# Weight sums formed by accumulating transfers instead of VectorE, in a two-layer streaming trunk

## The chip, the cores and the metric

The kernel runs on one core of one Trainium2 chip. A time is in device microseconds (us) for one execution of the whole program; of several runs the median is given. TensorE is called PE, its weight loads PEld, VectorE DVE, ScalarE ACT, GpSimd POOL; SP is the sequencer that issues nearly all DMA transfers here.

## The reference

One sequence of 512 rows of width 2048 goes through two layers in float32. The first is an mLSTM mixer (8 heads), the second a chunked band attention (16 heads) that reads one shared K and V. Nearly all the work is matrix products of 512 rows with weights that are read once:

```
proj = h @ w_in                        # layer 1: 2048 x 20496
qk = silu(causal_conv(proj[..., :A_V0], conv_w, conv_b))
ht = mlstm_chunkwise(q, k, v, li, lf)
y = sigmoid(o) * rmsnorm(ht) * silu(z);   x = x + gate * rmsnorm(y @ w_out)
kv = hkv @ kv_w                        # 2048 x 4096, shared
qz = h @ w_in                          # layer 2: 2048 x 4096
o = chunk_band_attention(q, k, v, rel_table)
x = x + gate * rmsnorm((o * silu(z)) @ w_out)
```

## The kernel before, in words

Each float32 operand is split into a rounded part (hi) and a rest (lo), and a product is three matmuls, hi hi, hi lo and lo hi (`mm3`, L276). `split` (L202) makes the two: ACT casts hi, DVE subtracts to get lo. All of these instructions carry line L203 in the profile.

The weights lie in DRAM in the order of use (`stream`, L73), cut into pieces of up to 128 x 1024 values. `wpiece` (L224) delivers the next piece: `raw_load` (L214) issues its transfer on SP into a `raw` tile, and `split` makes `wh` and `wl` of it. There are two `raw` buffers (RAW_BUFS) and in some stages a third one that a stage lends (`spare`), and three each of `wh` and `wl`. The planner puts a piece's load and its splits ahead by a fixed number of instructions (AHEAD) in each engine's order; on each engine instructions then run in that order, and a waiting one holds up those behind it.

Three stages form products of 2 x 2 blocks with seven block products instead of eight (`proj_s`, L319): the rows' halves against pairs of row tiles and column tiles of the weights, with sums formed before and after. They are the heads of layer 1 from the fourth on (query and key pairs, output and gate pairs; pool `hq`), the shared keys (pool `zx`) and the query and gate pairs of layer 2 (pool `kq`). For these, `wpiece` is called with `groups`: for each group of one or two pairs of row tiles, three DVE instructions form block sums of the weights. Of the blocks r0, r1, r2, r3 of a piece, L244 forms (r1 - r0, r2 - r1) into a tile `ws`, L245 puts r2 - r1 + r0 in place of r1 in the raw tile, and L246 forms the third sum, r3 minus that, into `ws`. Then `ws` too is split, into `wsh` and `wsl`. `ws` has one buffer in the heads and two in the keys and the attention, `wsh` and `wsl` have two.

The same heads' values (`proj_b` with `summed`, L295) use one difference of two row tiles' weights (L251, `diff`), for the row halves whose inputs were summed.

The inputs' side of the seven products is summed by DVE in `half_sums` (L379) and `three_sums` (L393); the products are put together after the last piece in `proj_s` (L367 to L377), from PSUM tiles D, C, A and B.

```
nc.vector.tensor_tensor(t[:, : 2 * w], r[:, w : 3 * w], r[:, : 2 * w], op=ALU.subtract)   # L244
nc.vector.tensor_tensor(r[:, w : 2 * w], t[:, w : 2 * w], r[:, :w], op=ALU.add)           # L245
nc.vector.tensor_tensor(t[:, 2 * w :], r[:, 3 * w :], r[:, w : 2 * w], op=ALU.subtract)   # L246
```

Of the kernel before, what the change touches and what calls it, by code (L numbers as in the profile page):

```python
# [46 lines left out]
ATT_PAIRS = 8  # L47
# [99 lines left out]
def hybrid_trunk(ctx, tc, xT, xN, c, adaT, cols, wst, wg, ext, kc, out):  # L147
    nc = tc.nc
# [62 lines left out]
    loads = []  # L211
    pin = tc.keep_in_program_order

    def raw_load(keep=lambda ins: ins):  # L214

        i, at = wpos
        n = sum(w for _, _, w in order[i][1])
        wpos[:] = i + 1, at + P * n
        own = spare[0] and i % (RAW_BUFS + 1) == 0
        raw = (spare[0] if own else wp).tile([P, 1024], F32, tag="raw", name=f"wr{i}", bufs=1 if own else RAW_BUFS)[:, :n]  # L220
        keep(nc.sync.dma_start(raw, wst[at : at + P * n].rearrange("(p n) -> p n", p=P)))
        loads.append(raw)

    def wpiece(mat, groups=(), pl=None, bufs=(2, 2), diff=False, early=False):  # L224

        if stock and not early:
            return stock.pop(0)()
        i = wpos[0] - len(loads)  # L230
        m, blocks = order[i]
        assert m == mat
        n = sum(w for _, _, w in blocks)
        with tc.high_priority(ahead[0]):
            if not loads:
                raw_load()
            raw = loads.pop(0)
            ts = []
            c0 = 0
            for j, ns in enumerate(groups):  # L240
                w = ns * P
                r = raw[:, c0 : c0 + 4 * w]
                t = pl.tile([P, 3 * w], F32, tag="ws", name=f"ws{i}_{j}", bufs=bufs[0])
                nc.vector.tensor_tensor(t[:, : 2 * w], r[:, w : 3 * w], r[:, : 2 * w], op=ALU.subtract)  # L244
                nc.vector.tensor_tensor(r[:, w : 2 * w], t[:, w : 2 * w], r[:, :w], op=ALU.add)  # L245
                nc.vector.tensor_tensor(t[:, 2 * w :], r[:, 3 * w :], r[:, w : 2 * w], op=ALU.subtract)  # L246
                ts.append(t)
                c0 += 4 * w
            if diff:
                t = pl.tile([P, n // 2], F32, tag="ws", name=f"ws{i}", bufs=1)  # L250
                nc.vector.tensor_tensor(t, raw[:, n // 2 :], raw[:, : n // 2], op=ALU.subtract)  # L251
                ts.append(t)
            hi = wp.tile([P, 1024], F32R, tag="hi", name=f"wh{i}")[:, :n]
            lo = wp.tile([P, 1024], F32R, tag="lo", name=f"wl{i}")[:, :n]
            if i == 0:
                pin(nc.scalar.copy(hi, raw))

                def rest():
                    parted[0] = nc.vector.tensor_tensor(lo, raw, hi.bitcast(F32), op=ALU.subtract)
                    behind(parted[0], first[0])  # L260
                    return [(hi, lo)]

                return rest
            parted[:] = split(hi, lo, raw, *first[1:] if i < 3 else ())
# [54 lines left out]
    def proj_s(mat, xs, ss, f, z1, z2, name, pl, bufs, at={}, merged=False, other=False):  # L319

        D, C, A, B = [(newa if other and n != "d" else newp)(f"ps_{n}{name}") for n in "dcab"]
        pieces = pair_pieces(f, merged)
        begun = set()
        h0, h1_ = slice(0, 256), slice(256, 512)
        for i, (sk, nk) in enumerate(pieces):
            if i in at:
                at[i]()
            main, *extra = wpiece(mat, [len(ks) for ks in sk], pl, bufs)  # L330

            def acc(ps, cols, parts, b, x, last):
# [12 lines left out]
            def seven(g, ks):  # L345
                ns = len(ks)
                b0 = 4 * sum(len(u) for u in sk[:g])
                end = i == len(pieces) - 1 and g == len(sk) - 1
                for ps, cols, t, at_, x, last in (
                    (D, h1_, 0, 1, lambda k: ss[k][1], False),  # L350
                    (D, h0, 0, 0, lambda k: xs[2 * k][:, :, h0], end),
                    (C, h0, 1, 1, lambda k: ss[k][2], False),
                    (C, h1_, 1, 0, lambda k: ss[k][0], end),
                    (A, h0, 0, 3, lambda k: xs[2 * k + 1][:, :, h0], False),
                    (A, h1_, 1, 2, lambda k: xs[2 * k + 1][:, :, h1_], end),
                    (B, h0, 0, 2, lambda k: ss[k][3], end),
                ):
                    if i == 0 and g == 0 and ps is B:
                        eight()
                    for j, k in enumerate(ks):  # L360
                        acc(ps, cols, extra[g] if t else main, (0 if t else b0) + at_ * ns + j, x(k), last and j == ns - 1)

            if i:
                eight()
            for g, ks in enumerate(sk):
                seven(g, ks)
        with tc.high_priority(AHEAD):  # L367
            nc.scalar.copy(z1[:, 0, :], D[:, h0])
            nc.vector.tensor_tensor(z2[:, 1, :], z1[:, 0, :], D[:, h1_], op=ALU.add)
            nc.vector.tensor_tensor(z1[:, 1, :], z2[:, 1, :], C[:, h0], op=ALU.add)  # L370
            nc.vector.tensor_tensor(z2[:, 0, :], z2[:, 1, :], C[:, h1_], op=ALU.add)
            nc.vector.tensor_tensor(z2[:, 1, :], z1[:, 1, :], C[:, h1_], op=ALU.add)
            nc.vector.tensor_tensor(z1, z1, A.rearrange("p (a t) -> p a t", a=2), op=ALU.add)
            if f < KT // 2:
                nc.vector.tensor_tensor(z2, z2, B.rearrange("p (a t) -> p a t", a=2), op=ALU.add)
            else:
                nc.vector.tensor_tensor(z2[:, 0, :], z2[:, 0, :], B[:, h0], op=ALU.add)  # L377

    def half_sums(raw, pl, tag, name, bufs, keep=lambda ins: ins):  # L379

        (a11, a21), (a12, a22) = ((r[:, :256], r[:, 256:]) for r in raw)
        keep(nc.vector.tensor_tensor(a11, a11, a21, op=ALU.subtract))
        nc.vector.tensor_tensor(a21, a21, a22, op=ALU.add)
        nc.vector.tensor_tensor(a22, a22, a11, op=ALU.subtract)
        nc.vector.tensor_tensor(a12, a12, a22, op=ALU.subtract)
        out = []
        for i, t in enumerate(raw):
# [5 lines left out]
    def three_sums(raw, pl, name, bufs, s1=None):  # L393
# [1 line left out]
        (a11, a21), (a12, a22) = ((r[:, :256], r[:, 256:]) for r in raw)  # L395
        nc.vector.tensor_tensor(a11, a11, a21, op=ALU.subtract)
        if s1 is not None:
            nc.vector.tensor_tensor(a21, a21, a22, op=ALU.add)
            split(s1[:, 0, :], s1[:, 1, :], a21)
        nc.vector.tensor_tensor(a22, a22, a11, op=ALU.subtract)  # L400
        nc.vector.tensor_tensor(a12, a12, a22, op=ALU.subtract)
        s3 = pl.tile([P, 2, 256], F32R, tag="s3", name=f"{name}_3", bufs=bufs)
        split(s3[:, 0, :], s3[:, 1, :], a11)
# [135 lines left out]
    h1 = []  # L539
# [177 lines left out]

    def pair(c, name, other, f=HEAD_PAIRS, at={}):
        z1, z2 = (acp.tile([P, 2, 256], F32, tag="so", name=f"{name}_{i}", bufs=6) for i in range(2))
        proj_s("a_w_in", h1, h1s, f, z1, z2, name, hq, (1, 2), at, True, other)  # L720
        return [z.rearrange("p a t -> p (a t)") for z in (z1, z2)]

    def scores(h, j, qk, pr, nm, nmd, tot):
# [377 lines left out]
    for i in range(KT // 2):  # L1101
# [2 lines left out]
        at = {2: input_sums} if ready < KT // 2 else {}  # L1104
        assert ready == KEY_PAIRS[i]
        spare[0] = zp
        proj_s("kv_w", hkv, hs, ready, z[:, 0:2, :], z[:, 2:4, :], f"k{i}", zx, (2, 2), at, True, i % 2 == 1)
        nc.sync.dma_start(ksc[i].rearrange("p a t -> p (a t)"), z.rearrange("p a t -> p (a t)"))
    zxst.close()
    kst.close()  # L1110
# [7 lines left out]
    for k in range(0, KT, 2):  # L1118
# [6 lines left out]
                raw[i], raw[i], amul[:, 2 * KT + c : 2 * KT + c + 1], mod[:, 48 + c : 49 + c], op0=ALU.mult, op1=ALU.add  # L1125
            )
        if k // 2 < ATT_PAIRS:
            nc.vector.tensor_tensor(raw[0][:, 256:], raw[0][:, 256:], raw[1][:, 256:], op=ALU.add)
# [25 lines left out]
    def queries(h, steps):  # L1154

        z1 = at.tile([P, 2, 256], F32, tag="zq", name=f"zq{h}")
        z2 = at.tile([P, 2, 256], F32, tag="z", name=f"z{h}", bufs=2)
        proj_s("b_w_in", h2, h2s, ATT_PAIRS, z1, z2, f"z{h}", kq, (2, 2), steps, True)
# [236 lines left out]
```

## Time and profile before

| what | us |
|---|---|
| median of 3 runs | 2782.41 |
| the runs | 2779.46, 2782.7, 2782.41 |
| span of the profiled execution, first to last instruction | 2780.8 |
| PE busy in it | 2757.6 |
| DVE busy in it | 2180.5 |
| ACT busy in it | 1388.8 |

The profiled execution's own time is not listed apart from its span; the median of the runs is 1.6 us above the span. A row of a group reads: line, engine, operation, what is written <- what is read, shapes, count | total busy us, mean ns of one | idle time of the engine just before, and what ended it. A row of waits reads: who waited <- for whom: us in total, times, longest. Buffer numbers are left out of tile names: `wr`, `wh`, `wl` are a piece's raw tile and its two parts, `ws`, `wsh`, `wsl` the block sums' tile and its parts; names that begin ps_ are PSUM tiles, and the letter after it is that of the product (d, c, a, b), with q, o, k, z for the stage (zq and zo in the heads, k in the keys, z in the attention).

### The profile page before, as it was taken

The page shows a single profiled execution, that of the slowest core. Times are in us where ns is not written, and L with a number is a line of the kernel's source. Part 1 is how long each engine was busy: PE and PEld are TensorE (multiplying, and loading weights), DVE is VectorE, ACT ScalarE, POOL GpSimd, SP SyncE. Part 2 cuts the span into 40 slices and gives each one's busy share as a digit, 9 for nine tenths or more (in the row PEclk, how much of TensorE's full clock was granted, in tenths as well). Part 3 has the DMA queues.
Part 4 walks back from the last instruction along what each step waited for, and adds up shares of the span by engine and source line. Part 5 has one row for each costly group of instructions (what it writes and reads, how often), then busy time and mean ns, then how long its engine had stood idle before and what let it go on. Part 6 is the DMA issues. An engine that isn't in the chain of part 4 may idle for free.

```text
span 2780.8 us, 41974 instructions
## 1 busy us (share of the span) xinstructions
PE 2757.6 (99%) x16186; PEld 2446.3 (88%) x16186; DVE 2180.5 (78%) x3421; ACT 1388.8 (50%) x1993; POOL 0.2 (0%) x4
## 2 busy tenths in 40 slices
PE   8999999999999999999999999999999999999998
PEld 6887888888998989989999888888998899999877
DVE  8975978669897887878878676567976788898666
ACT  4243624234554554555645334568534466666523
POOL 0000000000000000000000000000000000000000
PEclk9999999999999999999999999999999999999999
DMA  9754687855233232232326799788535534334686
GB/s 367 292 202 136 246 303 265 300 205 195 92 116 106 100 123 98 101 116 102 120 93 215 236 293 301 250 269 286 175 130 187 162 129 129 125 124 129 214 308 243
DMA packets 167874, 527.05 MB, mean 190 GB/s; under 512 B 17989, under 2 KB 33893, under 8 KB 155001
## 3 DMA queue, kind: packets, MB, share of 16 engines
q1 hardware_dynamic: 167674, 524.38, 54.6%
q8 instruction: 126, 2.06, 0.3%
q14 instruction: 74, 0.61, 0.1%
HBM read 490.69 MB, written 38.85 MB: 190 GB/s over the span
## 4 chain that ended last, share of the span: by engine, by line
PE 91%; DVE 5%; DMA 3%; issue 1%; ACT 1%; SPq 0%; DVEq 0%; ACTq 0%
PE ps_y L274 17%; PE ps_v L274 12%; PE ps_kv L274 5%; PE ps_azo L274 5%; PE ps_o L274 4%; PE ps_czo L274 3%; PE ps_dzo L274 3%; PE ps_az L274 3%; PE ps_cz L274 3%; PE ps_dz L274 3%; PE ps_qk L274 3%; PE ps_z L274 3%; PE ps_l L274 3%; PE ps_bzo L274 3%; PE ps_s L274 2%; PE ps_n L274 2%
## 5 line engine op out<-in xcount | busy, mean ns | idle before, releaser
L203 ACT CAST wh<-wr 128x1024 fp32r<-128x1024 f32 (+1 forms) x560 | 580.0, 1037 | 734.9 <-PE ps_y L274 217.0
L203 DVE TENSOR_TENSOR wl<-wr,wh 128x1024 fp32r<-128x1024 f32 (+1 forms) x560 | 674.5, 1206 | 337.2 <-ACT wh L203 335.6
L274 PE MATMUL ps_y<-wh,y 128*128 128x512 f32 x1536 | 476.7, 390 | 0.5 <-ACT sqy L927 0.5
L274 PEld LDWEIGHTS ps_y<-wh,y 128*128 128x128 f32 x1536 | 288.2, 188 | 60.8 <-ACT sqy L927 1.0
L203 ACT CAST wsh<-ws 128x768 fp32r<-128x768 f32 (+2 forms) x236 | 178.8, 757 | 260.4 <-PE ps_az L274 124.0
L274 PE MATMUL ps_y<-wl,y 128*128 128x512 f32 x768 | 299.0, 389 | 0.0
L274 PE MATMUL ps_v<-wh,h 128*128 128x512 f32 x912 | 289.6, 390 | 0.0
L203 DVE TENSOR_TENSOR wsl<-ws,wsh 128x768 fp32r<-128x768 f32 (+2 forms) x236 | 203.0, 860 | 72.8 <-ACT wsh L203 71.3
L445 DVE CUSTOM_DVE_ANT_0 ada<-ada,scB,cl 128x2048 f32<-128x2048 f32 (+1 forms) x96 | 222.6, 2325 | 18.3 <-DMA ada<-in_adaT 18.3
L274 PEld LDWEIGHTS ps_v<-wh,h 128*128 128x128 f32 x912 | 171.2, 188 | 34.9
L274 PE MATMUL ps_v<-wl,h 128*128 128x512 f32 x456 | 177.9, 390 | 0.0
L274 PEld LDWEIGHTS ps_y<-wl,y 128*128 128x128 f32 x768 | 144.3, 188 | 29.3
L274 PE MATMUL ps_kv<-wh,hkv 128*128 128x512 f32 x512 | 159.3, 390 | 0.0
L244 DVE TENSOR_TENSOR ws<-wr 128x256 f32<-128x256 f32 (+1 forms) x208 | 133.1, 640 | 7.2 <-DMA wr<-in_wst 5.3
L274 PEld LDWEIGHTS ps_kv<-wh,hkv 128*128 128x128 f32 x512 | 96.1, 188 | 19.7
L274 PEld LDWEIGHTS ps_v<-wl,h 128*128 128x128 f32 x456 | 85.7, 188 | 17.8 <-issue 0.9
L274 PE MATMUL ps_kv<-wl,hkv 128*128 128x512 f32 x256 | 99.7, 390 | 0.0
L274 PE MATMUL ps_l<-h,wh 128*128 128x512 f32 x320 | 98.5, 390 | 0.0
L246 DVE TENSOR_TENSOR ws<-wr 128x128 f32<-128x128 f32 (+1 forms) x208 | 83.0, 399 | 4.0
L245 DVE TENSOR_TENSOR wr<-ws,wr 128x128 f32<-128x128 f32 (+1 forms) x208 | 82.6, 397 | 2.9
L274 PE MATMUL ps_azo<-h,wh 128*128 128x256 f32 (+1 forms) x372 | 84.1, 314 | 0.0
L274 PE MATMUL ps_qk<-h,wh 128*128 128x512 f32 x256 | 79.3, 390 | 0.0
(408 smaller groups left out, 6354.1 us busy)
## 6 DMA issues: line engine op xcount, KB each, us to landing
wr<-in_wst SPq DMA_DIRECT2D x530, 512.0 KB, 3.5
ada<-in_adaT SPq DMA_DIRECT2D x94, 1024.0 KB, 6.3
ada<-in_adaT SPq DMA_DIRECT2D x36, 512.0 KB, 7.6
adq<-in_adaT SPq DMA_DIRECT2D x64, 256.0 KB, 4.7
xt<-nsc SPq DMA_DIRECT2D x48, 256.0 KB, 4.3
wr<-in_wst SPq DMA_DIRECT2D x26, 384.0 KB, 3.1
yr<-ysc SPq DMA_DIRECT2D x28, 256.0 KB, 7.1
bsc<-in_ext SPq DMA_DIRECT2D x16, 320.0 KB, 5.1
```

Source lines behind the costliest of these rows:

```text
L203: ins = nc.scalar.copy(hi, src), nc.vector.tensor_tensor(lo, src, hi.bitcast(F32), op=ALU.subtract)
L244: nc.vector.tensor_tensor(t[:, : 2 * w], r[:, w : 3 * w], r[:, : 2 * w], op=ALU.subtract)
L245: nc.vector.tensor_tensor(r[:, w : 2 * w], t[:, w : 2 * w], r[:, :w], op=ALU.add)
L246: nc.vector.tensor_tensor(t[:, 2 * w :], r[:, 3 * w :], r[:, w : 2 * w], op=ALU.subtract)
L274: return nc.tensor.matmul(ps, a, b, start=start, stop=stop)
L445: pin(nc.vector.tensor_tensor_reduce(c, c, (sc or scB)[:, j * w : (j + 1) * w], 1.0, mod[:, i : i + 1] if j else col(CB + i), ALU.mult, AL ...
```

## The change

L244 and L251 go. In their place `raw_load` makes the `ws` tile when it loads the piece: one transfer on SP brings the left blocks from DRAM, and a second, issued on POOL, adds the right blocks from DRAM to what is in the tile (`accum_op`). The piece itself is loaded as before. Since such a transfer adds and does not subtract, the block sums have the other sign, r1 + r0 and r2 + r1, and the signs move: the weights' third sum and, on the rows' side, some sums in `half_sums`, `three_sums` and the attention's inputs turn from plus to minus or back, and so do three of the sums after the products. `ws` has three buffers in the heads and four in the keys and the attention; the values' difference, now a sum, has three. The scratch space for the descriptors of POOL's transfers is set to 4096 bytes of a partition.

```diff
-    def raw_load(keep=lambda ins: ins):
+    def raw_load(keep=lambda ins: ins, groups=(), pl=None, bufs=1, diff=False):
         i, at = wpos
         n = sum(w for _, _, w in order[i][1])
         wpos[:] = i + 1, at + P * n
+        src = wst[at : at + P * n].rearrange("(p n) -> p n", p=P)
+        pairs, c0 = [], 0
+        for j, ns in enumerate(groups):
+            w = ns * P
+            t = pl.tile([P, 3 * w], F32, tag="ws", name=f"ws{i}_{j}", bufs=bufs)
+            keep(nc.sync.dma_start(t[:, : 2 * w], src[:, c0 : c0 + 2 * w]))
+            nc.gpsimd.dma_start(t[:, : 2 * w], src[:, c0 + w : c0 + 3 * w], accum_op=ALU.add)
+            pairs.append(t)
+            c0 += 4 * w
+        if diff:
+            t = pl.tile([P, n // 2], F32, tag="ws", name=f"ws{i}", bufs=bufs)
+            keep(nc.sync.dma_start(t, src[:, : n // 2]))
+            nc.gpsimd.dma_start(t, src[:, n // 2 :], accum_op=ALU.add)
+            pairs.append(t)
...
-        keep(nc.sync.dma_start(raw, wst[at : at + P * n].rearrange("(p n) -> p n", p=P)))
-        loads.append(raw)
+        keep(nc.sync.dma_start(raw, src))
+        loads.append((raw, pairs))
...
-                nc.vector.tensor_tensor(t[:, : 2 * w], r[:, w : 3 * w], r[:, : 2 * w], op=ALU.subtract)
                 nc.vector.tensor_tensor(r[:, w : 2 * w], t[:, w : 2 * w], r[:, :w], op=ALU.add)
-                nc.vector.tensor_tensor(t[:, 2 * w :], r[:, 3 * w :], r[:, w : 2 * w], op=ALU.subtract)
+                nc.vector.tensor_tensor(t[:, 2 * w :], r[:, 3 * w :], r[:, w : 2 * w], op=ALU.add)
...
-            if diff:
-                t = pl.tile([P, n // 2], F32, tag="ws", name=f"ws{i}", bufs=1)
-                nc.vector.tensor_tensor(t, raw[:, n // 2 :], raw[:, : n // 2], op=ALU.subtract)
-                ts.append(t)
...
-            nc.vector.tensor_tensor(z2[:, 1, :], z1[:, 0, :], D[:, h1_], op=ALU.add)
+            nc.vector.tensor_tensor(z2[:, 1, :], z1[:, 0, :], D[:, h1_], op=ALU.subtract)
             nc.vector.tensor_tensor(z1[:, 1, :], z2[:, 1, :], C[:, h0], op=ALU.add)
-            nc.vector.tensor_tensor(z2[:, 0, :], z2[:, 1, :], C[:, h1_], op=ALU.add)
-            nc.vector.tensor_tensor(z2[:, 1, :], z1[:, 1, :], C[:, h1_], op=ALU.add)
+            nc.vector.tensor_tensor(z2[:, 0, :], C[:, h1_], z2[:, 1, :], op=ALU.subtract)
+            nc.vector.tensor_tensor(z2[:, 1, :], C[:, h1_], z1[:, 1, :], op=ALU.subtract)
...
-        proj_s("a_w_in", h1, h1s, f, z1, z2, name, hq, (1, 2), at, True, other)
+        proj_s("a_w_in", h1, h1s, f, z1, z2, name, hq, (3, 2), at, True, other)
...
-        proj_s("kv_w", hkv, hs, ready, z[:, 0:2, :], z[:, 2:4, :], f"k{i}", zx, (2, 2), at, True, i % 2 == 1)
+        proj_s("kv_w", hkv, hs, ready, z[:, 0:2, :], z[:, 2:4, :], f"k{i}", zx, (4, 2), at, True, i % 2 == 1)
...
-    nc = bacc.Bacc("TRN2", target_bir_lowering=False, num_devices=1)
+    nc = bacc.Bacc("TRN2", target_bir_lowering=False, num_devices=1, dynamic_dma_scratch_size=4096)
```

The attention's call of `proj_s` changes from (2, 2) to (4, 2) likewise; the sign changes at L384, L385, L398, L400 and L1128 are single words.

More of the change, by code (lines that the diff above doesn't have):

```diff
@@ L218, in raw_load, with wpiece @@
         wpos[:] = i + 1, at + P * n
+        src = wst[at : at + P * n].rearrange("(p n) -> p n", p=P)
[12 more added lines that the diff above has]
+            pairs.append(t)
         own = spare[0] and i % (RAW_BUFS + 1) == 0
         raw = (spare[0] if own else wp).tile([P, 1024], F32, tag="raw", name=f"wr{i}", bufs=1 if own else RAW_BUFS)[:, :n]
-        keep(nc.sync.dma_start(raw, wst[at : at + P * n].rearrange("(p n) -> p n", p=P)))
-        loads.append(raw)
-    def wpiece(mat, groups=(), pl=None, bufs=(2, 2), diff=False, early=False):
+        keep(nc.sync.dma_start(raw, src))
+        loads.append((raw, pairs))
+    def wpiece(mat, groups=(), pl=None, bufs=(3, 2), diff=False, early=False):
         if stock and not early:
@@ L235, in wpiece @@
             if not loads:
-                raw_load()
-            raw = loads.pop(0)
-            ts = []
+                raw_load(groups=groups, pl=pl, bufs=bufs[0], diff=diff)
+            raw, ts = loads.pop(0)
             c0 = 0
-            for j, ns in enumerate(groups):
+            for t, ns in zip(ts, groups):
                 w = ns * P
                 r = raw[:, c0 : c0 + 4 * w]
-                t = pl.tile([P, 3 * w], F32, tag="ws", name=f"ws{i}_{j}", bufs=bufs[0])
-                nc.vector.tensor_tensor(t[:, : 2 * w], r[:, w : 3 * w], r[:, : 2 * w], op=ALU.subtract)
                 nc.vector.tensor_tensor(r[:, w : 2 * w], t[:, w : 2 * w], r[:, :w], op=ALU.add)
-                nc.vector.tensor_tensor(t[:, 2 * w :], r[:, 3 * w :], r[:, w : 2 * w], op=ALU.subtract)
-                ts.append(t)
+                nc.vector.tensor_tensor(t[:, 2 * w :], r[:, 3 * w :], r[:, w : 2 * w], op=ALU.add)
                 c0 += 4 * w
-            if diff:
-                t = pl.tile([P, n // 2], F32, tag="ws", name=f"ws{i}", bufs=1)
-                nc.vector.tensor_tensor(t, raw[:, n // 2 :], raw[:, : n // 2], op=ALU.subtract)
-                ts.append(t)
             hi = wp.tile([P, 1024], F32R, tag="hi", name=f"wh{i}")[:, :n]
@@ L382, in half_sums @@
         keep(nc.vector.tensor_tensor(a11, a11, a21, op=ALU.subtract))
-        nc.vector.tensor_tensor(a21, a21, a22, op=ALU.add)
-        nc.vector.tensor_tensor(a22, a22, a11, op=ALU.subtract)
+        nc.vector.tensor_tensor(a21, a21, a22, op=ALU.subtract)
+        nc.vector.tensor_tensor(a22, a22, a11, op=ALU.add)
         nc.vector.tensor_tensor(a12, a12, a22, op=ALU.subtract)
@@ L397, in three_sums @@
         if s1 is not None:
-            nc.vector.tensor_tensor(a21, a21, a22, op=ALU.add)
+            nc.vector.tensor_tensor(a21, a21, a22, op=ALU.subtract)
             split(s1[:, 0, :], s1[:, 1, :], a21)
-        nc.vector.tensor_tensor(a22, a22, a11, op=ALU.subtract)
+        nc.vector.tensor_tensor(a22, a22, a11, op=ALU.add)
         nc.vector.tensor_tensor(a12, a12, a22, op=ALU.subtract)
@@ L1127, in hybrid_trunk @@
         if k // 2 < ATT_PAIRS:
-            nc.vector.tensor_tensor(raw[0][:, 256:], raw[0][:, 256:], raw[1][:, 256:], op=ALU.add)
+            nc.vector.tensor_tensor(raw[0][:, 256:], raw[0][:, 256:], raw[1][:, 256:], op=ALU.subtract)
             h2s[k // 2][0] = h2[k][:, :, 256:]
@@ L1157, in queries @@
         z2 = at.tile([P, 2, 256], F32, tag="z", name=f"z{h}", bufs=2)
-        proj_s("b_w_in", h2, h2s, ATT_PAIRS, z1, z2, f"z{h}", kq, (2, 2), steps, True)
+        proj_s("b_w_in", h2, h2s, ATT_PAIRS, z1, z2, f"z{h}", kq, (4, 2), steps, True)
         zq, sz = (z.rearrange("p a t -> p (a t)") for z in (z1, z2))
```

## The prediction

> **What bounds the kernel now.** I read the page's busy shares first, then the stretches in which the changed lines run, then who TensorE (PE) waited for in them, then the groups of matmuls by form.
>
> ```profile
> span 2780.8 us, 41974 instructions
> PE 2757.6 (99%) x16186; PEld 2446.3 (88%) x16186; DVE 2180.5 (78%) x3421; ACT 1388.8 (50%) x1993; POOL 0.2 (0%) x4
> ...
> L244 DVE TENSOR_TENSOR ws<-wr 128x256 f32<-128x256 f32 (+1 forms) x208 | 133.1, 640 | 7.2 <-DMA wr<-in_wst 5.3
> ```
>
> PE is busy for all but 23.2 us of the span (2780.8 - 2757.6). The line that goes, L244, is VectorE (DVE) work, and DVE has 600 us free. L244 runs only in three stretches: the heads' sevenfold products, the keys' and the attention's. The windows view gives them, in this order (us; then busy time of PE, PEld, DVE, ACT, POOL; granted clock; DMA share; GB/s):
>
> ```profile
> 676.00:1497.00 821.00, 819.62 (x5561) 763.49 (x5560) 672.03 (x1083) 440.87 (x582) 0.00 (x0) 1.00 0.31 107
> 1946.00:2100.00 154.00, 153.22 (x1242) 151.41 (x1242) 131.35 (x218) 67.68 (x86) 0.00 (x0) 1.00 0.43 151
> 2166.00:2575.00 409.00, 409.00 (x3194) 399.92 (x3193) 364.13 (x769) 259.53 (x436) 0.00 (x0) 1.00 0.41 131
> ```
>
> In the three, 1384 us together, PE is idle for 1384.00 - 1381.84, that is 2.2 us, at clock 1.00. DVE is the second busiest, 82 to 89% of each, and PE hardly waits for it. What PE and its weight loads waited for between 676 and 2575 us:
>
> ```profile
> PE ps_dzq L274 <- DVE wl L203: 1.1, 3, 0.4
> PE ps_dk L274 <- DVE wl L203: 0.8, 1, 0.8
> PE ps_x L973 <- DVE xn L965: 0.5, 1, 0.5
> ...
> PEld ps_dzq L274 <- DVE wl L203: 2.6, 6, 0.6
> PEld ps_dk L274 <- DVE wl L203: 1.0, 1, 1.0
> ```
>
> Those that a less loaded DVE can end are ps_dzq (a head's first query pair, where DVE also has the convolution) and ps_dk (the first key pair): 1.1 + 0.8 = 1.9 us on PE, or 2.6 + 1.0 = 3.6 us if the whole wait of the weight loads counts. Since a matmul's end is modelled, lateness can also hide in a form's mean:
>
> ```profile
> L274 PE MATMUL ps_bz<-h2s,wh 128*128 128x256 f32 x256 | 53.3, 292 | 0.0
> L274 PE MATMUL ps_dz<-h2s,wh 128*128 128x256 f32 x256 | 51.9, 295 | 0.0
> ...
> L274 PE MATMUL ps_dz<-h,wh 128*128 128x256 f32 x256 | 50.3, 287 | 0.0
> ...
> L274 PE MATMUL ps_cz<-h,wsh 128*128 128x256 f32 x256 | 48.8, 283 | 0.0
> ```
>
> Most 256-column forms have 283 ns; three of the attention's exceed it by 9, 12 and 4 ns, over 256 instructions 2.3 + 3.1 + 1.0 = 6.4 us. Other work stands between those matmuls (transposes, scores), so I don't put this down to DVE, but it is the most that can hide there. The ceiling of the gain is 3.6 + 6.4 = 10 us.
>
> **The change, part by part.**
>
> *Removed:* L244, 208 times, 133.1 us, and L251, whose one-line view is
>
> ```profile
> L251 DVE TENSOR_TENSOR ws<-wr x28: 682/685/692, 825.0 to 1389.4; 128x512 f32<-128x512 f32 x28
> ```
>
> 28 x 0.685 = 19.2 us. DVE loses 152 us, all beside PE. For the end that is worth what PE's named waits lose. Each piece of weights loses 0.69 us of DVE, or 0.42 us in the small form, ahead of its wl. The longest ps_dzq wait is 0.4 us (0.6 on the weight load), so these go; the ps_dk wait of 0.8 to 1.0 us shrinks to 0.1 to 0.3 us. Next late there is ScalarE's (ACT) cast wh, which also waited behind L245. I take -2 us, between 0 and -3.6.
>
> *Moved signs:* L246, L369 to L372, L384 to L398 and L1128 keep their number, shapes and operands' places, only add and subtract change: nothing.
>
> *Added on SP:* 236 loads of the left operand (208 + 28), 256 KB each, 128 KB for a small group. Each stands in the queue ahead of its piece's own load. *Added on POOL:* 236 accumulating transfers of the same size. Each waits for its load's landing; behind it stand only later accumulations, since POOL has nothing else to do (x4 above). *Added wait:* L245 now waits for an accumulation as well as for wr. Behind L245 on DVE stand the piece's wl and wsl, and the evacuations L369 to L375, for which PE waits next.
>
> So the question is whether the chain (load, accumulation, L245, wh, wl, wsl) is early enough. In one stretch of the heads, DVE's own timeline and SP's read (start, us, engine, line; A to D are successive pieces):
>
> ```profile
> 904.81 1.23 DVE L203 TENSOR_TENSOR wl<-wr,wh 128x1024 fp32r<-128x1024 f32 x1 [0.70 <-ACT wh L203]
> 905.95 0.95 DVE L203 TENSOR_TENSOR wsl<-ws,wsh 128x768 fp32r<-128x768 f32 x1
> ...
> 908.85 1.23 DVE L203 TENSOR_TENSOR wl<-wr,wh 128x1024 fp32r<-128x1024 f32 x1 [0.83 <-ACT wh L203]
> ...
> 917.81 0.69 DVE L244 TENSOR_TENSOR ws<-wr 128x512 f32<-128x512 f32 x1
> 918.53 0.43 DVE L245 TENSOR_TENSOR wr<-ws,wr 128x256 f32<-128x256 f32 x1
> ...
> 920.27 1.23 DVE L203 TENSOR_TENSOR wl<-wr,wh 128x1024 fp32r<-128x1024 f32 x1 [0.86 <-ACT wh L203]
> ```
>
> ```profile
> 906.06 0.33 SPq L221 DMA_DIRECT2D wr<-in_wst  x1
> ```
>
> Piece A's wl ends at 906.04, and that frees the raw buffer for the load of piece C at 906.06: two raw buffers. Piece A's wsl ends at 906.90. With three ws buffers in the heads, piece D's left operand can be issued then, directly behind C's raw load. Piece D's L245 starts at 918.53, and without L244 it could at 917.81. So the load and the accumulation have 917.8 - 906.9 = 10.9 us. The durations (median us from issue to landing):
>
> ```profile
> wr<-in_wst SPq DMA_DIRECT2D x530, 512.0 KB, 3.5
> ...
> xt<-in_xT SPq DMA_DIRECT2D x4, 1024.0 KB, 9.1
> ...
> kt<-ksc SPq DMA_DIRECT2D x16, 256.0 KB, 2.7
> ...
> yr<-ysc SPq DMA_DIRECT2D x28, 256.0 KB, 7.1
> ```
>
> The load takes 2.7 us (kt, same size, same kind of stretch), which leaves 8.2 us for the accumulation. A second way agrees: a piece with two pairs of rows is 42 matmuls, and PE starts 3194 in 409 us in the third stretch, 0.128 us apiece, 5.4 us a piece; three ws buffers make a loop of 16.1 us, of which load 2.7, L245 0.43, wh 1.05 (the cast's mean is 1037 ns in the page's first group), wl 1.23, wsl 0.95 and some 0.5 of handing over leave 9.3 us. The keys and the attention have four ws buffers, so one period more.
>
> No row shows an accumulating transfer. It moves 256 KB and reads the destination besides: not under kt's 2.7 us, and at most, I take it, xt's 9.1 us, four times the bytes on a loaded fabric. I take 5 us: wr's 3.5 (512 KB, as many bytes as are read here) and 1.5 for a queue and engine that does nothing now. That is 3 us inside the 8.2. The Trainium skill, "DMA: Bandwidth & Descriptors", Anatomy of one DMA, fits 2.0 us + bytes / 436e3 for a transfer issued on GpSimd, an estimate of 2.6 us for 256 KB; by it there would be 5.6 us to spare and the sum would stay. No run here shows that for an accumulation.
>
> ```profile
> L203 ACT CAST wh<-wr 128x1024 fp32r<-128x1024 f32 (+1 forms) x560 | 580.0, 1037 | 734.9 <-PE ps_y L274 217.0
> ```
>
> *DMA engines:* their share is 0.31 in the heads, 0.43 in the keys. The keys have 30 pieces in 154 us, 5.1 us each, so 2.2 us of engine time a piece; the load adds about half of a raw load's, 0.8 us (0.31 of 5.2 us in the heads is 1.6, nearly all raw loads), the accumulation 0.8 at least: 3.8 of 5.1 us. Hidden, unless an accumulation costs the engines much more (rival 3).
>
> *Sum:* 2780.8 - 2 = 2778.8 us of span. The median of the runs shown, 2782.41, is 1.6 us over the span (they reach from 2779.46 to 2782.7), so the forecast is **2780.5 us**, own range 2777 to 2784. About 0.2% (5.6 us) is what a measurement of this kernel can tell from no change.
>
> **The rivals.**
>
> 1. *More than the named waits goes*: the lateness in the attention's means was DVE's too. Against it: no wait there is put down to DVE. Its time is 2782.4 - 10 = 2772 if all goes, 2776 if most does.
>
> 2. *The accumulation lands late* (slower). Place: L245 in the heads, where three ws buffers give the shortest loop. Point: an accumulation of over 8.2 us. Each us beyond delays a loop of three pieces, a third of a us a piece; the heads have 112 sevenfold pieces (208 - 32 of the keys - 64 of the attention), so 37 us for each us. At the 9.1 us bound: 0.9 x 37 = 33 us, 2816 us; just past the point, 2790. For it: yr's 256 KB took 7.1 us when the engines were busy. Against: the share is 0.31 here. The Trainium skill, "SBUF — State Buffer", SBUF: two separate sides, warns that DVE in its two-port modes keeps GpSimd from writing descriptors, which speaks against putting these transfers on POOL; it would stretch this rival's term. DVE's groups at the top of the page are TENSOR_TENSOR, which the same page exempts; no run here has such a transfer to test it on.
>
> 3. *The DMA engines become the bound* (slower). Point, from the shares above: the keys have 5.1 - 2.2 - 0.8 = 2.1 us of engine time for an accumulation, the heads 5.2 - 1.6 - 0.8 = 2.8. If it is 3.0 us (nearly four times a plain transfer of its size), the keys lose 30 x 0.9 = 27 us and the heads 140 x 0.2 = 28 us: 2837 us.
>
> 4. *SP's order* (slower, small). SP spends most of its time in front of a raw load:
>
> ```profile
> SPq L221 <- DVE wl L203: 1367.8, 415, 16.5
> ...
> SPq L1169 <- DVE mx L1186: 79.2, 15, 5.6
> ```
>
> Now a left operand's load that waits for a ws buffer stands in front of raw loads, the heads' stores and the attention's kt, vt and bias; and where bias waits (79.2 us, 15 times) the load and the accumulation behind it start late together. One piece late by 1 us for 10 of the 16 attention heads: +10, 2790 us.
>
> That the change doesn't relieve DVE at all is excluded, since L244 and L251 are gone; that it relieves it without an effect is the forecast's upper end.
>
> **How the numbers follow.** Forecast (hidden) 0.50; rival 1 0.10; rival 2 0.18; rival 3 0.14; rival 4 0.08. Faster by over 0.2% is rival 1: 0.10. Same: 0.50. Slower: 0.18 + 0.14 + 0.08 = 0.40. The range takes in rival 4, rival 2 to its bound of 2816 and the better end of rival 3, and of rival 1 half: **2775 to 2826 us**, leaving out some 0.05 below and 0.13 above.
>
> **What would show it.** Right: DVE's busy time down by some 150 us, L245 with no idle time put down to an accumulation worth naming, PE busy within 1 us of the three stretches, the accumulation's landing at 4 to 6 us. Rival 2: L245's idle time <- DMA ws, PE waits for wl in the heads alone. Rival 3: DMA share near 1 in the keys, and raw loads far over 3.5 us. Rival 4: PE waits at the attention's head boundaries. The prediction is wrong if an accumulation lands after more than 8 us, or occupies the engines for over 2 us.

## The result, and the profile after

The changed kernel takes **2953.64 us** (median of 4 runs, 2951.24 to 2954.41) against 2782.44 us of the kernel before on the same chip: a ratio of 1.062, 95% interval 1.0605 to 1.0632. The forecast was 2780.5 us, and the range ended at 2826.

The page of the changed kernel, in the rows that answer to those shown of before (L256 is the old L245; L224 and L225 are the load of the left operand on SP and the accumulation on POOL):

```profile
span 2951.3 us, 42851 instructions
PE 2801.8 (95%) x16186; PEld 2477.3 (84%) x16186; DVE 2037.7 (69%) x3185; ACT 1388.4 (47%) x1993; POOL 205.3 (7%) x240
...
q1 hardware_dynamic: 201658, 581.41, 59.1%
q0 software_dynamic: 33984, 57.03, 12.2%
...
L256 DVE TENSOR_TENSOR wr<-ws,wr 128x128 f32<-128x128 f32 (+1 forms) x208 | 83.0, 399 | 407.7 <-DMA ws<-in_wst 251.0
...
ws<-in_wst SPq DMA_DIRECT2D x199, 256.0 KB, 4.2
ws<-in_wst POOLq DMA_DIRECT2D x199, 256.0 KB, 4.8
```

DVE's busy time fell by 143 us (2180.5 to 2037.7), as the change intends, and an accumulation lands after 4.8 us, where 5 was predicted. But L256 now stands still for 407.7 us, where L245, in the kernel before, has 2.9 us in all:

```profile
L245 DVE TENSOR_TENSOR wr<-ws,wr 128x128 f32<-128x128 f32 (+1 forms) x208 | 82.6, 397 | 2.9
```

PE was idle for 23.2 us of the span and is now for 149.5 (2951.3 - 2801.8).

The stages tell where. The windows view of the heads (from their first sevenfold matmul to the last head's end), of the keys and of the attention (us; busy time of PE, PEld, DVE, ACT, POOL; granted clock; DMA share; GB/s), first of the kernel before, then of the changed one:

```profile
695.00:1502.00 807.00, 805.62 (x5502) 752.00 (x5500) 658.12 (x1050) 434.88 (x569) 0.00 (x0) 1.00 0.32 108
1946.00:2109.00 163.00, 162.22 (x1317) 160.41 (x1317) 135.96 (x225) 69.43 (x88) 0.00 (x0) 1.00 0.42 149
2196.00:2586.00 390.00, 390.00 (x3152) 386.06 (x3152) 348.60 (x752) 251.37 (x431) 0.00 (x0) 1.00 0.42 133
```

```profile
694.00:1595.00 901.00, 825.72 (x5503) 766.41 (x5502) 571.52 (x916) 435.59 (x574) 117.01 (x135) 0.97 0.64 169
2046.00:2248.00 202.00, 177.34 (x1318) 173.01 (x1319) 117.08 (x196) 69.19 (x87) 24.29 (x28) 0.92 0.72 191
2335.00:2757.00 422.00, 400.15 (x3151) 390.57 (x3150) 313.76 (x690) 252.25 (x431) 50.57 (x58) 0.99 0.74 195
```

The heads lose 94 us, the keys 39, the attention 32: 165 of the 170.5 us by which the span grew. In these rows PE's idle time (stretch less busy) goes from 2.2 to 121.8 us, and its busy time from 1357.8 to 1403.2 us for the same matmuls. So about 120 us are waits, and 45 us are matmuls that run longer, most of it at a lower granted clock: it is 0.97, 0.92 and 0.99 in the stages in which PE now stops again and again.

What PE and DVE waited for in the changed kernel (who <- for whom: us in total, times, longest):

```profile
DVE wr L256 <- DMA ws<-in_wst: 251.0, 67, 6.7
...
DVE wr L256 <- DMA wr<-in_wst: 156.4, 55, 5.2
...
PE ps_n L280 <- DVE zo L869: 39.4, 5, 11.5
```

```profile
PE ps_czo L280 <- DVE wsl L203: 28.3, 13, 4.4
PE ps_ck L280 <- DVE wsl L203: 24.0, 10, 4.3
PE ps_t L1204 <- DVE s L1195: 21.9, 27, 3.0
```

L256 waits 67 times for its accumulation and 55 times for the piece's raw load. The stages differ: in the heads it waits 168.6 us for accumulations and 94.3 us for raw loads, in the keys 76.1 us for accumulations alone, and in the attention (2335 to 2757 us) for raw loads alone:

```profile
DVE wr L256 <- DMA wr<-in_wst: 58.7, 18, 5.2
```

PE waits for the parts of the block sums (wsl), and for other DVE work that stands behind L256 (zo at a head's end, the scores' s).

The timelines of the changed kernel in the keys show how an accumulation of 4.8 us comes late. First DVE (start, us, engine, line):

```profile
2124.12 0.43 DVE L256 TENSOR_TENSOR wr<-ws,wr 128x256 f32<-128x256 f32 x1 [5.98 <-DMA ws<-in_wst]
...
2126.92 0.95 DVE L203 TENSOR_TENSOR wsl<-ws,wsh 128x768 fp32r<-128x768 f32 x1
...
2129.72 0.95 DVE L203 TENSOR_TENSOR wsl<-ws,wsh 128x768 fp32r<-128x768 f32 x1
...
2138.00 0.42 DVE L256 TENSOR_TENSOR wr<-ws,wr 128x256 f32<-128x256 f32 x1 [6.20 <-DMA ws<-in_wst]
```

then SP and POOL:

```profile
2127.90 0.33 SPq L224 DMA_DIRECT2D ws<-in_wst  x1
...
2130.70 0.33 SPq L224 DMA_DIRECT2D ws<-in_wst  x1
```

```profile
2131.74 0.86 POOL L225 DMA_DIRECT2D ws<-in_wst  x1 [9.90 <-DMA ws<-in_wst]
```

A left operand's load is issued at 2127.90, the moment a wsl has ended (2126.92 + 0.95) and given its ws buffer back. The load lands, POOL issues the accumulation at 2131.74, that lands, and L256 runs at 2138.00. From the L256 at 2124.12, which waited too, to this one are 13.9 us, in which two pieces went through; PE needs 5.1 us for one. The wsl at 2126.92 belongs not to the piece whose L256 ran at 2124.12 but to one two pieces earlier: it stood in DVE's order behind that waiting L256. So in the keys a ws buffer comes free only after a later piece's accumulation has landed.

### The profile page after: what moved, and what is told of

It reads as the page before. It is cut to its first block, busy times and chain, and to the rows that moved or that the text cites. A ratio compares the mean times of both kernels' runs of the same rounds, so it can differ in the third digit from the quotient of the medians.

```text
span 2951.3 us, 42851 instructions
## 1 busy us (share of the span) xinstructions
PE 2801.8 (95%) x16186; PEld 2477.3 (84%) x16186; DVE 2037.7 (69%) x3185; ACT 1388.4 (47%) x1993; POOL 205.3 (7%) x240
## 3 DMA queue, kind: packets, MB, share of 16 engines
q0 software_dynamic: 33984, 57.03, 12.2%
## 4 chain that ended last, share of the span: by engine, by line
PE 35%; DMA 16%; DVE 9%; issue 3%; ACT 1%; SPq 0%; DVEq 0%; POOLq 0%; ACTq 0%
PE ps_y L280 17%; DMA ws<-in_wst 10%; DMA wr<-in_wst 5%; PE ps_kv L280 4%; PE ps_v L280 2%; DVE wl L203 2%; PE ps_dz L280 2%; PE ps_cz L280 2%; PE ps_az L280 2%; DVE wsl L203 1%; DMA xt<-nsc 1%; PE ps_o L280 1%; PE ps_bz L280 1%; PE ps_s L280 1%; DMA ada<-in_adaT 1%
## 5 line engine op out<-in xcount | busy, mean ns | idle before, releaser
L256 DVE TENSOR_TENSOR wr<-ws,wr 128x128 f32<-128x128 f32 (+1 forms) x208 | 83.0, 399 | 407.7 <-DMA ws<-in_wst 251.0
L225 POOL DMA_DIRECT2D ws<-in_wst x208 | 180.8, 876 | 2379.8 <-DMA ws<-in_wst 1075.1
L280 PE MATMUL ps_n<-p,v 128*128 128x512 f32 (+3 forms) x352 | 70.4, 366 | 39.4 <-DVE zo L869 39.4
L280 PEld LDWEIGHTS ps_n<-p,v 128*128 128x128 f32 x352 | 63.9, 215 | 46.7 <-DVE zo L869 40.4
```

Source lines behind the costliest of these rows:

```text
L225: nc.gpsimd.dma_start(t[:, : 2 * w], src[:, c0 + w : c0 + 3 * w], accum_op=ALU.add)
L280: return nc.tensor.matmul(ps, a, b, start=start, stop=stop)
```

## The experiments

**Theory 1 (T1), the loop through DVE's order.** The planner fixes the order of DVE's instructions. How many later pieces' L256 (L245) stand there ahead of a piece's wsl, counted in the instruction order of each kernel, I call the lead. A ws buffer that comes free serves a later piece only after the L256 of as many pieces as the lead, so the pieces that are really in the loop are the ws buffers less the lead. For most pieces:

| kernel | ws buffers (heads, keys, attention) | lead | pieces in the loop |
|---|---|---|---|
| before | 1, 2, 2 | 0, 1, 1 | (sums need no transfer of their own) |
| changed, e4 | 3, 4, 4 | 1, 2, 1 to 2 | 2, 2, 2 to 3 |
| e1 | 3, 4, 4 | 1, 2, 1 to 2 | (as before) |
| e2, e7 | 3, 4, 4 | 0, 0, 0 | 3, 4, 4 |
| e3 | 5, 6, 6 | 1, 2, 1 to 2 | 4, 4, 4 to 5 |
| e5 | 3, 2, 2 | 1, 1, 1 | (as before) |
| e6 | 4, 5, 5 | 2, 3, 2 to 3 | 2, 2, 2 to 3 |
| e8 | 2, 2, 2 | 0, 0, 0 | 2, 2, 2 |
| e9 | 4, 5, 5 | 0, 0, 0 | 4, 5, 5 |

Raw buffers make a second loop of this kind: a piece's wl gives its raw buffer back, and wl too can stand behind a later piece's L256. It does so for 56 of the heads' 112 pieces, 29 of the keys' 32 and 20 of the attention's 64 in the changed kernel, for 2, 3 and 3 before, 24, 29 and 16 in e1, and 2, 0 and 2 in e2 (counted in DVE's order in the traces).

In the kernel before, the lead cost nothing, because L244 and L245 needed only the raw load, and that was released by wl.

**The rivals:** the accumulation itself is too slow or occupies the DMA engines too much, whatever the order; or the signs and the larger buffer numbers cost time without any transfer. Each diff is against the changed kernel, but for that of e5.

### e1: signs and buffers alone

```diff
-            keep(nc.sync.dma_start(t[:, : 2 * w], src[:, c0 : c0 + 2 * w]))
-            nc.gpsimd.dma_start(t[:, : 2 * w], src[:, c0 + w : c0 + 3 * w], accum_op=ALU.add)
...
+                nc.vector.tensor_tensor(t[:, : 2 * w], r[:, w : 3 * w], r[:, : 2 * w], op=ALU.add)
                 nc.vector.tensor_tensor(r[:, w : 2 * w], t[:, w : 2 * w], r[:, :w], op=ALU.add)
```

The values' sum likewise; signs and buffer numbers stay as changed.

> The changed kernel with its signs, buffers and descriptor space, but DVE forms the block sums again (adding) and POOL issues nothing. Every theory: the time of before, 2782 us within 8; if it is over 2800, the moved signs or the extra buffers cost something by themselves and the transfers are not the whole cause.

Measured: 2790.97 us (2789.29 to 2792.68), ratio 1.0035 (1.0021 to 1.0048). That is 10 us over the kernel before on the same chip, a little outside the 8 us that were expected. Without the transfers 161 of the 171 us are gone, so signs and buffers alone are not the main cause. The 10 us come from the attention. Its window there, and two rows of waits of e1:

```profile
2192.00:2596.00 404.00, 395.02 (x3147) 385.34 (x3145) 348.23 (x749) 252.97 (x430) 0.00 (x0) 1.00 0.42 128
```

```profile
DVE ws L252 <- DMA wr<-in_wst: 66.9, 38, 3.5
```

```profile
PE ps_t L1203 <- DVE s L1194: 8.0, 13, 1.5
```

The attention takes 404 us against 390, and L252 (the sum that L244 formed) waits 66.9 us for raw loads, 30.5 of them in the attention, where L244 of before waited 5.3 in all. With four ws buffers the lead in e1's order is the changed kernel's (2 in the keys, 1 to 2 in the attention), so DVE stands early in front of a piece that hasn't landed, and the scores' s, for which PE waits, stands behind it. That this is the reason is argued from these rows; e2 tests it. The changed kernel's attention has the same kind of wait, for raw loads and not for accumulations (58.7 us), and loses 32 us where e1 loses 14.

### e2: the changed kernel with one edge more in DVE's order

```diff
-                nc.vector.tensor_tensor(r[:, w : 2 * w], t[:, w : 2 * w], r[:, :w], op=ALU.add)
+                first_sum = nc.vector.tensor_tensor(r[:, w : 2 * w], t[:, w : 2 * w], r[:, :w], op=ALU.add)
+                if c0 == 0 and last_split:
+                    behind(first_sum, last_split[0])
...
-                split(sh, sl, t)
+                last_split[:] = split(sh, sl, t)
```

The edge puts a piece's first L256 behind the wsl of the piece before. Transfers, buffers and waits stay.

> The changed kernel with one tie more: on DVE the first sum of a piece (L256) stands behind the last split (wsl) of the piece before. Theory 1 (loop: in DVE's order L256 of piece p, which waits for an accumulation, stands ahead of the splits wl and wsl of pieces p-1 and p-2, which free the buffers that the next loads wait for, so that load and accumulation of only about two pieces overlap): with the splits ahead of it the time falls to 2780 to 2810 us, and DVE's waits of L256 for ws fall from 251 us to under 60. Theory 2 (the DMA engines, or the accumulation's own pace, are the bound): the same traffic in nearly the same time, 2920 to 2960 us.

Measured: **2787.86 us** (2785.93 to 2790.41), ratio 1.0025 (1.0016 to 1.0035). It is 7 us over the kernel before on the same chip, so 164 of the 171 us are back, with the transfers of the changed kernel. Rows of e2's page and waits, and its windows of the keys and the attention:

```profile
PE 2757.4 (99%) x16186; PEld 2447.5 (88%) x16186; DVE 2052.5 (74%) x3185; ACT 1395.2 (50%) x1993; POOL 204.7 (7%) x240
...
q0 software_dynamic: 33984, 57.03, 12.9%
...
ws<-in_wst SPq DMA_DIRECT2D x199, 256.0 KB, 4.5
ws<-in_wst POOLq DMA_DIRECT2D x199, 256.0 KB, 5.4
```

```profile
DVE wr L256 <- DMA ws<-in_wst: 13.6, 12, 6.0
```

```profile
1950.00:2115.00 165.00, 164.90 (x1320) 162.98 (x1321) 120.72 (x197) 69.92 (x87) 24.24 (x28) 0.98 0.85 236
2202.00:2592.00 390.00, 390.00 (x3153) 386.07 (x3152) 317.59 (x690) 255.18 (x430) 50.23 (x58) 1.00 0.79 211
```

The accumulation lands later than in the changed kernel (5.4 us against 4.8) and yet L256 waits 13.6 us instead of 251.0. The DMA engines are busier (0.85 in the keys, against 0.72), and the keys take 165 us, near before's 163. So neither the landing nor the engines' load is the cause by itself; the order is. The attention takes before's 390 us with the moved signs and four ws buffers, so what e1 lost there was the order too, and not the signs. What is left is mostly one wait of 5.3 us at the keys' start (PE ps_dk <- ACT wh).

### e3: two more ws buffers in each stage

The buffer numbers (3, 2), (4, 2), (4, 2) become (5, 2), (6, 2), (6, 2).

> The changed kernel with two ws buffers more in each stage (5 in the heads, 6 in the keys and the attention), order as the planner makes it. Theory 1: in the keys and the attention the load of a piece is no longer held by the split behind L256, PE idle there falls from 34 us to under 10; in the heads the raw loads (two raw buffers) still wait for wl behind L256, so half of the 65 us there stays: 2820 to 2880 us. Theory 2: 2930 to 2960 us.

Measured: 2872.16 us (2870.34 to 2877.42), ratio 1.0329 (1.0313 to 1.0344): about half of the loss is back. The waits of e3:

```profile
DVE wr L256 <- DMA wr<-in_wst: 285.2, 122, 5.6
```

The waits for ws have nearly gone (8.5 us are left), but now the raw load is late 122 times. In the heads 73 of 112 pieces have one later L256 ahead of their wl, which frees one of two raw buffers, so a single piece is in that loop. The windows of the keys and the attention:

```profile
1994.50:2165.50 171.00, 167.11 (x1318) 163.46 (x1319) 117.43 (x196) 68.32 (x87) 22.55 (x27) 0.98 0.81 225
2252.00:2675.00 423.00, 398.33 (x3152) 388.06 (x3150) 312.43 (x687) 252.50 (x431) 49.08 (x56) 1.00 0.72 192
```

In the keys PE's idle time fell from 24.7 to 3.9 us. In the attention it did not fall: 423 us and 24.7 us idle, against 422 and 21.9 in the changed kernel, where under 10 us for both stages was expected. So the ws buffers were not what held the attention. The extra ws buffers help the one loop and not the other, and the time stays where the second one puts it.

### e4: the transfer on POOL overwrites instead of adding

```diff
-            nc.gpsimd.dma_start(t[:, : 2 * w], src[:, c0 + w : c0 + 3 * w], accum_op=ALU.add)
+            nc.gpsimd.dma_start(t[:, : 2 * w], src[:, c0 + w : c0 + 3 * w])
```

The left operand of the block sums is thereby left out of the result; the waits are those of the changed kernel.

> The changed kernel with POOL's transfers overwriting instead of adding: the block sums' left operands are left out, all waits and bytes from DRAM stay. Theory 1: the chain is shorter by what the addition costs, about 1 us of 4.8; a loop of two pieces of about 13.9 us loses 1 us, so 2900 to 2930 us. Theory 2 in its form that the addition itself is slow: 2780 to 2820 us.

Measured: 2863.53 us (2854.39 to 2868.39), ratio 1.029 (1.0266 to 1.0313). The page of e4:

```profile
q0 software_dynamic: 17696, 57.03, 6.4%
...
ws<-in_wst SPq DMA_DIRECT2D x199, 256.0 KB, 3.6
ws<-in_wst POOLq DMA_DIRECT2D x199, 256.0 KB, 3.6
```

This lies outside both expected ranges. A plain transfer in the same place still costs 83 us, so the adding isn't the whole cause. Half of the loss goes with it, since the chain in the loop is shorter by 1.8 us in the two landings (3.6 + 3.6 against 4.2 + 4.8); I had expected less of that. The prediction's own sum, done again with a loop of two pieces, gives the size: two pieces are 2 x 5.37 = 10.7 us, of which L256, wh, wl, wsl and handing over take 4.2, and 6.6 are left for both landings. They take 9.0 us in the changed kernel, 2.4 too many for two pieces, over 112 pieces up to 135 us (measured in the heads: 94); in e4 they take 7.2, 0.6 too many, 34 us (measured: 840 - 807 = 33). The sum gives the size and no more, and that it meets 33 so closely is luck: not every piece has the lead, and in e4's heads L256 waits longer for raw loads (109.9 us) than for accumulations (65.2 us), which the sum leaves out.

```profile
694.00:1534.00 840.00, 812.84 (x5502) 758.91 (x5501) 572.84 (x916) 437.85 (x574) 72.50 (x135) 0.98 0.55 181
```

### e5: the kernel before with three ws buffers in the heads

```diff
-        proj_s("a_w_in", h1, h1s, f, z1, z2, name, hq, (1, 2), at, True, other)
+        proj_s("a_w_in", h1, h1s, f, z1, z2, name, hq, (3, 2), at, True, other)
```

This is an edit of before: DVE forms the sums, no transfer is added. The values' difference has three buffers too, and the scratch space is the changed kernel's.

> The kernel before with one edit: three ws buffers in the heads instead of one (and the smaller descriptor space, to have room); DVE forms all sums. In the run where DVE formed the sums with the changed kernel's buffers, the heads ended 5 us earlier than before and the attention took 10 us more. If the heads' part comes from the ws buffers there, this one has 2774 to 2779 us; if it came from the planner's other order, 2780 to 2786 us.

Measured: **2776.2 us** (2774.32 to 2778.25), ratio 0.9981 (0.9972 to 0.999). It is the fastest of all kernels here, ahead of both. The heads' window:

```profile
695.00:1497.00 802.00, 802.00 (x5497) 750.40 (x5496) 650.07 (x1052) 436.83 (x570) 0.00 (x0) 1.00 0.34 110
```

PE is never idle there; before, the same stretch took 807 us. What there was to gain in the heads can be had by buffers, with no work taken from DVE. The planner's order moved with them here too (lead 1 in place of 0), so the buffers are not shown apart from the order.

### e6: a third raw buffer and one more ws buffer

RAW_BUFS becomes 3, the ws buffers 4, 5, 5, and the scratch space 2048, to make room.

> The changed kernel with three raw buffers instead of two and 4, 5 and 5 ws buffers in the heads, the keys and the attention (descriptor space 2048 bytes, to have room), order as the planner makes it. Theory 1 (loops through the buffers that are freed by splits behind L256): the run with two raw buffers and 5, 6, 6 ws buffers had 2872 us and waited 285 us in L256 for raw loads; here those waits fall under 100 us and the time to 2790 to 2840 us. Theory 2 (the DMA engines): 2860 us or more.

Measured: 2959.62 us (2954.78 to 2962.3), ratio 1.0638 (1.0623 to 1.0652). The expectation failed: as slow as the changed kernel. The order explains it, though I read it only afterwards: with more buffers the planner put L256 one piece further ahead (lead 2 in the heads, 3 in the keys), and the loop is again of two pieces. The waits for raw loads fell from e3's 285.2 us to 130.8, not under 100, and those for accumulations are 277.4 us. DVE's and SP's timelines of e6 in the keys repeat the picture above:

```profile
2124.99 0.43 DVE L256 TENSOR_TENSOR wr<-ws,wr 128x256 f32<-128x256 f32 x1 [6.30 <-DMA ws<-in_wst]
...
2137.07 0.42 DVE L256 TENSOR_TENSOR wr<-ws,wr 128x256 f32<-128x256 f32 x1 [6.06 <-DMA ws<-in_wst]
```

```profile
2126.77 0.33 SPq L224 DMA_DIRECT2D ws<-in_wst  x1
...
2129.57 0.33 SPq L224 DMA_DIRECT2D ws<-in_wst  x1
```

From one waiting L256 to the next are 12.1 us for two pieces, with five ws buffers instead of four. An explanation found afterwards needs a run of its own, which is e9.

### e7: the order of e2, and the first two pieces of the keys by DVE

```diff
-            keep(nc.sync.dma_start(t[:, : 2 * w], src[:, c0 : c0 + 2 * w]))
-            nc.gpsimd.dma_start(t[:, : 2 * w], src[:, c0 + w : c0 + 3 * w], accum_op=ALU.add)
+            if i not in by_dve:
+                keep(nc.sync.dma_start(t[:, : 2 * w], src[:, c0 : c0 + 2 * w]))
+                nc.gpsimd.dma_start(t[:, : 2 * w], src[:, c0 + w : c0 + 3 * w], accum_op=ALU.add)
...
+                if i in by_dve:
+                    nc.vector.tensor_tensor(t[:, : 2 * w], r[:, w : 3 * w], r[:, : 2 * w], op=ALU.add)
```

> The kernel with the tie that puts L256 behind the splits of the piece before, and with the sums of the first two key pieces formed by DVE (no transfer for these two). PE waited 5.3 us there for wh, behind an accumulation that had begun 5 us before it was wanted. Theory 1: that wait goes, 2780 to 2785 us. If something else sets the start of the keys, 2786 to 2790 us.

Measured: 2782.57 us (2781.24 to 2785.12), ratio 1.0005 (0.9996 to 1.0013), the same as before. The wait at the keys' start is 1.0 us instead of 5.3, and 5 us are gone. The page's row of busy times:

```profile
PE 2756.2 (99%) x16186; PEld 2445.8 (88%) x16186; DVE 2053.5 (74%) x3187; ACT 1394.8 (50%) x1993; POOL 203.1 (7%) x238
```

and its windows of the heads and the keys:

```profile
695.00:1500.00 805.00, 803.18 (x5497) 750.58 (x5497) 579.49 (x913) 436.98 (x571) 116.79 (x135) 1.00 0.72 188
1944.00:2111.00 167.00, 164.71 (x1321) 161.52 (x1321) 120.56 (x197) 70.41 (x88) 25.99 (x30) 1.00 0.85 237
```

DVE has 127 us less to do than before (2180.5 - 2053.5), the waits that the change brought are nearly gone, and the time is before's: 2 us less in the heads (805 against 807), 4 more in the keys (167 against 163). In the heads e5, without any relief, takes 802. So the change, even mended, buys nothing that can be measured here.

### e8: the order of e2 with two ws buffers everywhere

> The kernel with the tie, and two ws buffers in each stage instead of 3, 4 and 4. Theory 1: load 4.5, accumulation 5.4 and the sums and splits that free the buffer some 4.5 us make about 14.5 us for two pieces, 7.2 us a piece where PE needs 5.1 to 6.4: about 2 us for each of 170 pieces of the heads and keys and 0.8 us for 64 of the attention, 3000 to 3200 us. If the buffers hardly matter once the order is right: 2785 to 2800 us.

Measured in one run, so without an interval: 3075.83 us, inside what was expected. Its page:

```profile
L256 DVE TENSOR_TENSOR wr<-ws,wr 128x128 f32<-128x128 f32 (+1 forms) x208 | 83.2, 400 | 459.1 <-DMA ws<-in_wst 454.7
```

With no lead, but only two buffers, the loop is of two pieces by the buffers alone, and L256 waits 454.7 us for ws. So what the edge in e2 gave was depth of the loop, and with the depth taken away again the loss is back.

### e9: e6 with the edge of e2

> The kernel of e6 (three raw buffers, ws buffers 4/5/5) and the tie of e2. If the loop has as many pieces as ws buffers less the lead of L256 over wsl in DVE's order, the tie sets the lead to zero in every stage, the loop has 4 and 5 pieces, and the time goes from e6's 2959.6 us to that of e2 or a little under: 2778 to 2790 us, L256's idle time behind ws under 30 us, PE busy at most 2765 us. If instead a third raw buffer itself costs (more loads in flight, transfers landing later, another place in SP's queue), it stays over 2850 us in spite of the order. If e2 gained for another reason than the loop (for example because the tie moves evacuations), it lies between.

Measured: 2785.64 us (2784.13 to 2789.86), ratio 1.0022 (1.0012 to 1.0032). The page of e9:

```profile
L256 DVE TENSOR_TENSOR wr<-ws,wr 128x128 f32<-128x128 f32 (+1 forms) x208 | 82.2, 395 | 11.6 <-DMA ws<-in_wst 6.1
```

The same buffers as in e6, another order: 174 us less, and 6.1 us of waits for ws in place of 277.4. The third raw buffer costs nothing by itself, and e6's failure was the order.

## Why the prediction was wrong

- **What bounds the kernel** held: PE. Once the order is mended, PE is busy for 99% again (e2, e7, e9).
- **Relief of DVE, -2 us**: not shown. DVE lost 143 us (127 in e7) where the sum had 152. The ps_dzq waits are gone in e2 and e7, but they go as well in e5, where DVE keeps all its work; the ps_dk wait, which was to shrink, is 1.0 us in e7 (5.3 in e2). The 5 us that e5 gains in the heads go with the ws buffers (one before, three there) and are more than the 2 to 3.6 us that I gave the relief.
- **Load 2.7 us, accumulation 5 us, bounds 2.7 to 9.1**: the accumulation measured 4.8 us, close to the 5; but 1.5 of the 5 had no row behind them, so that is partly luck. The load measured 4.2 instead of 2.7; in these stages it runs beside a raw load and an accumulation (DMA share 0.64 to 0.74), and the prediction went by kt's row. Together they take 9.0 us, less than the 10.9 that the prediction had for them: e2, with three pieces in the heads' loop, hides 9.9 us (4.5 and 5.4).
- **The failed step**: "three ws buffers make a loop of 16.1 us", hence 8.2 us for the accumulation, and "the keys and the attention have four ws buffers, so one period more". It counted buffers. The loop has as many pieces as buffers less the lead of L256 over wsl in DVE's order: two in the heads and in the keys, 10.7 us and 10.2. The two landings and the work between them need over 13. Behind L245 the prediction saw only the piece's own wl and wsl, and not those of earlier pieces. I read the order in the heads of before, where one ws buffer allows no lead, and carried it over to a kernel with three; in the keys and the attention of before the lead was already one. The ws buffers that were to give the accumulation time were spent on the lead.
- **The attention** lost 32 us in another loop, which the prediction left out. Its two to three pieces were enough for the accumulations, for which L256 waits nowhere there. The 32 us are the order's too (e2 has none of them), but L256 waits for raw loads; that the raw buffers' loop does this is argued from the lead of wl and from e3, and no run changes that loop alone.
- **Rival 1** (lateness hidden in the attention's means) is not borne out: the attention takes 390 us before and in e2, where DVE is busy for 31 us less of it (317.59 against 348.60).
- **Rival 2** named the right place and wait (L245 <- DMA ws) and the wrong condition: it asked for an accumulation of over 8.2 us, and 4.8 was enough. Its loss of a third of a us a piece was a half, and it was not confined to the heads. POOL's issue of an accumulation took 0.87 us, at the least as at the median, so no hold-up of its descriptors by DVE shows.
- **Rival 3, the DMA engines**: not reached. An accumulation costs 12.2% of 2951.3 us over 236 transfers, 1.53 us of engine time, under the point of 2.1; in e2 the keys run at a share of 0.85 in 165 us.
- **Rival 4, SP's order**: e2 and e9 leave all transfers on SP as they are, and they lie 7 and 5 us over the kernel before, most of which is the wait at the keys' start (5.3 and 5.5 us). It decided little.
- **The moved signs at nothing**: right. e1 lost 14 us in the attention, but e2, with the same signs and buffer numbers and another order, takes before's 390 us there.
- **The clock** was in no step: 45 of the 165 us are matmuls that run longer, some 35 of them by stretches at half clock after stalls (last section). What lengthens the others is open.

## What to carry to other kernels

A buffer is free when its last reader has run, and on an engine that works in order the last reader can stand behind an instruction that waits for a later buffer. So count the depth of a prefetch (how many pieces are under way at once) as the buffers less that lead, for each kind of buffer on the path, and read the lead in the changed kernel's order, since more buffers can change it. When work is moved from an engine to a transfer, the engine's instruction that uses the result gets a new wait: look at what stands behind it before counting what was saved.

## What the runs showed of the hardware

- **An accumulating transfer costs twice the engine time of a plain one.** The queue q0 took 12.2% of the 16 engines' time in 2951.3 us for 236 accumulations, 1.53 us each, and in e4 6.4% of 2861.6 us for the same 57.03 MB without adding, 0.78 us each. It has 33984 packets against 17696, lands after 4.8 us against 3.6, and POOL is busy with one issue for 0.87 us against 0.54 (medians of 236 issues). The Trainium skill, "DMA: Bandwidth & Descriptors", Anatomy of one DMA, fits 2.0 us + bytes / 436e3, an estimate of 2.6 us for 256 KB; the plain transfer beside other traffic took 3.6, the accumulation 4.8, and the measurement decides.
- **PE loses twice when it stalls.** In the changed kernel's keys PE is idle for 24.7 us and its matmuls take 15.1 us longer (177.34 against 162.22), at a granted clock of 0.92. The clock record of its trace has 18 stretches at half clock between 694 and 2757 us, 99 us together, all whole multiples of 3.41 us on one grid. PE is busy in 70 us of them, so they cost some 35 us, an estimate. Each begins behind 3.41 us of that grid in which PE was idle for a share of 0.56 to 1.00; stretches of the grid with a share up to 0.50 were followed by none. The shortest stall that set one off lasted 1.8 us. The Trainium skill, "TensorE: Matmul & The Clock Gate", Part 1: The HAM clock gate, states that an idle window of about 3.4 us halves the clock until about as long a busy one. The trace agrees on the length and on the half; but a window that was idle for a little over half was enough here, and the measurement decides.
- **More buffers can gain nothing or lose.** One more raw buffer and one more ws buffer in each stage changed 2953.6 us to 2959.6 (e6), because the order moved with them; one edge in the order then made 2785.6 of it (e9).
